# A two-layer mixer with a modulated block on one core: 256-byte tile lines, four-head latent queries, earlier output-gate panels, gating transposes in other banks

## The chip, the cores and the metric

The kernel runs on one core of one Trainium2 chip. The metric is the time of one execution on the device in microseconds (us). The kernel before was timed in 3 runs; their median is 2477.08 us, from 2476.04 to 2478.45.

## What is computed

512 tokens of width 1024 (fp32) go through two layers of one kind and one block of another. What matters here, cut from the reference:

```
def first_block(x, ...):                 # two layers
    for l in range(DEPTH):
        h = rmsnorm(x, g_pre_mix[l])
        (c_q, c_kv, k_r, p_in, s_u, s_v, cv_b, cv_c, cv_x, gate_logits) = split_cols(h @ w_in[l])
        y_a = mla_branch(c_q, c_kv, k_r, ...) @ w_br_a[l]      # q = rmsnorm(c_q) @ w_uq, 8 heads of 96
        y_b = pool_branch(p_in, ...) @ w_br_b[l]
        y_c = sgu_branch(s_u, s_v, ...) @ w_br_c[l]            # u * (masked 128 x 128 mix of rmsnorm(v))
        y_d = conv_branch(cv_b, cv_c, cv_x, ...) @ w_br_d[l]
        merged = sum of sigmoid(gate_logits) * (y_a, y_b, y_c, y_d)
        x = x + rmsnorm(merged @ w_out[l], g_post_mix[l])
        h = rmsnorm(x, g_pre_ffn[l])
        x = x + rmsnorm((silu(h @ w_ffn_gate[l]) * (h @ w_ffn_up[l])) @ w_ffn_down[l], g_post_ffn[l])

def second_block(x, c, ctx, c_ctx, w_mod, ...):
    sh1, sc1, g1, sh2, sc2, g2 = split(silu(c) @ w_mod + b_mod)     # and the same for c_ctx
    h = rmsnorm(x) * (1 + sc1) + sh1
    (q_na, k_na, v_na, q_g, k_g, v_g, og, z_lr, m_a, m_b) = split(h @ w_in)
    mix = merge(neighborhood attention(q_na, k_na, v_na), gated linear attention(q_g, k_g, v_g), silu(og), ...) @ w_out
    x = x + g1 * mix
    x = x + g2 * swiglu(modulated rmsnorm(x), w_ffn_gate, w_ffn_up, w_ffn_down)
```

## The kernel before, in words

The 512 tokens are 4 tiles of 128 rows, the width is 8 steps k of 128. Every large product is made of fp32r matmuls on operands split in a high and a low part (`split`): `mm3` issues three matmuls for each k, high x high, high x low, low x high. `fm` takes a weight panel as the stationary operand and the transposed activations as the moving one; `tm` the other way round. In the trace a matmul reads `out<-moving,stationary`: `pg<-wh,mTh` moves a weight panel over the stationary merged activations.

Weights come in panels of up to 128 x 1024 elements (`panel`, `wsplit`, L273 to L300): SP starts the load into one of 2 raw buffers `wr`, ACT casts it to `wh` (L261), DVE subtracts to get `wl` (L262); `wh` and `wl` have 4 buffers each. Work beside the main stream ("thread a") has raw buffers of its own, also 2, which it shares with the w_mod loads.

TensorE's order is written out: `inorder` (L247) chains every matmul and transpose to the one recorded before it. Side work is a list of items of several steps; `tick`, called every 4 k of a main product, lets the next steps in, 1.5 for a tick in the layers' mixing stage. The other engines' orders come from the scheduler, and each runs its own in order. PSUM has eight banks: `g` (3) for main products, `s` (2), `tp` (2) and `po` (1) for side work; `self.ps("t")` gives a main-stream caller a `g` bank, a side-work caller a `tp` bank.

A layer mixes in this order: latent projections; then the main stream computes conv, pool and SGU branches, each followed by its gate products and its branch product (`gates`; the branch output `brh`/`brl` is the moving operand), while MLA runs beside it: values, queries, keys, scores, softmax, probabilities times values, in four pairs of heads `hp` and four query tiles `j`. Queries (L755 to L784) load a 192-column panel of `w_uq` for each pair and make two calls, each for two token tiles: 2 x 2 x 3 matmuls of 192 columns. Scores (L802) read the pair's `qT`. Then `w_out` (`mTh`, `mTl` stationary) and the FFN; the last 8 of the 22 pairs of FFN activations lie in a pool `keep`, the others in `drop`. A generator with the modulation rows of the second block (L1066 on: load 128 x 512 of w_mod on SP, multiply-add on DVE, L1076 and L1078) fills in behind the MLA items and in the FFNs.

In the SGU branch `turned` transposes the gated halves, 8 transposes of 128 x 128, into two banks from `self.ps("t")` (L946), then splits them into `brh`/`brl`.

In the second block, keys and values of the neighborhood attention are projected in a loop over panels (L1168 to L1175); each value tile goes to DRAM (`vd`) in 8 writes of 32 rows on SP (L1540). Then four output-gate products follow, each with its panel requested right before it (L1182 to L1186).

Tiles come from pools through `Aligned.tile` (L94 to L111), which pads a tile's bytes in a partition to a multiple of 128. The pool of small constants adds up to 2688 bytes, ten and a half lines of 256, and pools stack on it.

Of the kernel before, what the change touches and what calls it, by code (L numbers as in the profile page):

```python
# [9 lines left out]
F32 = mybir.dt.float32  # L10
# [7 lines left out]
P = 128  # L18
# [21 lines left out]
CTX = 256  # L40
PHASE = 0
WARM = 12
HIGH = ((0, 0), (1, 0), (0, 1))
# [50 lines left out]
class Aligned:  # L94
# [5 lines left out]
    def tile(self, shape, dt, **kw):  # L100
        size = 2 if dt == BF16 else 4
        n = math.prod(shape[1:])
        if n * size % P == 0:
            return self.pool.tile(shape, dt, **kw)
        line = P // size
        t = self.pool.tile([shape[0], -(-n // line) * line], dt, **kw)[:, :n]
        if len(shape) == 2:
            return t
        names = "abc"[: len(shape) - 1]
        spaced = " ".join(names)  # L110
        return t.rearrange(f"p ({spaced}) -> p {spaced}", **dict(zip(names[1:], shape[2:])))  # L111


class Builder:
# [620 lines left out]
    def mla(self, l, o, q, kv):  # L735
# [18 lines left out]

        def queries(hp, t2):  # L755
            if t2 == 0:
                wqs[hp] = self.panel(a["w_uq"][l], 0, 2, hp * 192, 192)
                qTs[hp] = q.tile([QK, 2, SEQ], F32, name=self.nm("qT"), tag="qT", bufs=2)
            wq, qT = wqs[hp], qTs[hp]
            ps = self.ps()  # L760
            for i in range(2):
                ts = slice((2 * t2 + i) * P, (2 * t2 + i) * P + P)
                for k in range(2):
                    self.mm3(ps[:, i * 192 : i * 192 + 192], (cT[0][:, k, ts], cT[1][:, k, ts]), (wq[0][:, k], wq[1][:, k]), k == 0, k == 1)
            four = lambda x, d: x.rearrange("p (t h d) -> p t h d", t=2, h=2)
            v = four(ps[:, :384], QK)
            qn = self.f2()
            qv = four(qn[:, :384], QK)
            nc.scalar.activation(qv[:, :, :, :64], v[:, :, :, :64], AF.Copy, scale=QK ** -0.5)
            rt = self.f2()  # L770
            ra, rb = four(rt[:, :128], ROPE), four(rt[:, 128:256], ROPE)
            tab = lambda x, lo, hi: x[:, 2 * t2 : 2 * t2 + 2, None, lo:hi].to_broadcast([P, 2, 2, hi - lo])
            nc.vector.tensor_tensor(ra, v[:, :, :, 64:96], tab(Cq, 0, 32), op=ALU.mult)
            nc.vector.tensor_tensor(rb[:, :, :, :16], v[:, :, :, 80:96], tab(Sq, 0, 16), op=ALU.mult)
            nc.vector.tensor_tensor(rb[:, :, :, 16:], v[:, :, :, 64:80], tab(Sq, 16, 32), op=ALU.mult)
            nc.vector.tensor_tensor(qv[:, :, :, 64:96], ra, rb, op=ALU.add)

            def turn():
                pt = self.ps("t")
                for i in range(4):  # L780
                    self.transpose(pt[:QK, i * P : i * P + P], qv[:, i // 2, i % 2], ident)
                nc.scalar.copy(qT.rearrange("p h (t n) -> p t h n", t=NT)[:, 2 * t2 : 2 * t2 + 2], pt[:QK].rearrange("p (t h n) -> p t h n", t=2, h=2))

            pTs["q", hp, t2] = turn  # L784

# [11 lines left out]
        def scores(hp, j):  # L797
            n = (j + 1) * P
            ps = []
            for i in range(2):  # L800
                s = self.ps()
                self.matmul(s[:, :n], qTs[hp][:, i, j * P : j * P + P], kTs[hp][:, i, :n], start=True, stop=True)  # L802
                nc.vector.memset(s[:64, n - 64 : n], NEG)
                ps.append(self.softmax(q, s, n, 4))
            pTs[hp, j] = ps
# [21 lines left out]

        def project(hp):
            return [[do(queries, hp, t2), lambda: None, lambda t2=t2: pTs.pop(("q", hp, t2))()] for t2 in range(2)] + [[do(keys, hp)]]

        items = [[do(values, t)] for t in range(NT)] + project(0) + [[]]
        for hp in range(4):
            more = project(hp + 1) if hp < 3 else []
            for j in range(NT):
                items.append([do(scores, hp, j), lambda: None, do(probs, hp, j), do(values_of, hp, j)])
                if more:
                    items.append(more.pop(0))
        return items
# [66 lines left out]
    def sgu_branch(self, l, w_in, hT, brp, q):  # L905
# [38 lines left out]
        def turned():  # L944
            for m in range(2):
                pt = self.ps("t")  # L946
                for t in range(NT):
                    self.transpose(pt[:, t * P : (t + 1) * P], cs[:, t, m * P : (m + 1) * P], ident)
                self.split(cT[0][:, m], cT[1][:, m], pt)
# [164 lines left out]
    def block2(self, hT, before):  # L1114
# [53 lines left out]
        for name, c0 in (("k", 512), ("v", 1024)):  # L1168
            pans = self.pans(w_in, c0)
            for h, n, nt in ((hcT, name + "c", 2), (hT, name, NT)):  # L1170
                for t in range(nt):
                    ps = self.tm(h, pans, t, 512)
                    with self.thread("a"):
                        na[n](t, ps)
# [7 lines left out]
        for m in range(4):  # L1182
            ps = self.fm(hT, self.panel(w_in, 0, KD, 2560 + m * P, P), 0)
            nc.scalar.activation(og[m], ps, AF.Tanh, scale=0.5)
# [481 lines left out]
```

## Time and profile before

| what | before |
|---|---|
| median of 3 runs | 2477.08 us |
| profiled execution, its own time | 2477.62 us |
| its span | 2475.8 us |
| instructions in the span | 30539 |
| TensorE busy (matmul) | 2450.2 us, 99% |
| VectorE (DVE) busy | 1232.1 us, 50% |
| ScalarE (ACT) busy | 851.2 us, 34% |
| GpSimd (POOL) busy | 73.4 us, 3% |
| moved by DMA | 279.72 MB, mean 113 GB/s |

The profile times one execution. Its span is the time from the first to the last instruction recorded; the execution's own time is 1.8 us more. A busy share is an average over all stages. Matmuls overlap: the end of one is modelled and lies after the start of the next, so that the pace of a stream is read from start to start, not from the durations. "Idle before" in an instruction's row is the time its engine stood before it and what ended that.

### The profile page before, as it was taken

To read this page: it belongs to the slowest core of one execution; us is meant where nothing else is said; L and a number is where in the kernel's file an instruction comes from. 1 tells how busy PE (TensorE), PEld (TensorE's weight loads), DVE (VectorE), ACT (ScalarE), POOL (GpSimd) and SP (SyncE) were. 2 spreads that over 40 slices of the span, in tenths; PEclk is the share of its full clock that TensorE was granted. 3 is DMA by queue.
4 is the path that set the end of the run, shared out by engine and by line. 5 is a ranking of instruction groups with operands and counts; after the bars stand their busy time and mean duration, and the time that the engine had idled before them with its cause. 6 is when DMAs were issued, how large, how long until landed. Compare 5 with 4: busy or idle time off the path is not lost.

```text
span 2475.8 us, 30539 instructions
## 1 busy us (share of the span) xinstructions
PE 2450.2 (99%) x12155; PEld 2017.2 (81%) x12155; DVE 1232.1 (50%) x2018; ACT 851.2 (34%) x1414; POOL 73.4 (3%) x113
## 2 busy tenths in 40 slices
PE   9999999999999999999999999999999999999999
PEld 7877788988888887778898888877877778988887
DVE  6456544566522645554455443275535646543323
ACT  4343433322322434343332222244434533322211
POOL 1000000000000100000000000020100000000000
PEclk9999999999999999999999999999999999999999
DMA  5323334345424432443435333451133225333323
GB/s 160 92 75 110 105 94 153 119 136 174 134 94 141 128 96 79 123 124 94 153 111 154 101 96 104 141 179 48 55 94 120 69 69 170 111 94 97 99 94 128
DMA packets 339376, 279.72 MB, mean 113 GB/s; under 512 B 28262, under 2 KB 282430, under 8 KB 339233
## 3 DMA queue, kind: packets, MB, share of 16 engines
q1 hardware_dynamic: 339233, 277.76, 37.6%
q8 instruction: 96, 1.57, 0.3%
q14 instruction: 47, 0.39, 0.0%
HBM read 262.27 MB, written 15.45 MB: 112 GB/s over the span
## 4 chain that ended last, share of the span: by engine, by line
PE 61%; DVE 3%; ACT 1%; issue 1%; DMA 1%; POOL 0%; DVEq 0%; ACTq 0%; POOLq 0%; SPq 0%
PE pg L252 47%; PE ps L252 6%; PE ppo L252 3%; PE ptp L252 3%; PE ptp L255 2%; DVE wl L262 1%; DMA wr<-in_w_mod 1%; ACT wh L261 0%; POOL sm L337 0%; DVE hn L361 0%; ACT p L847 0%; DVE xt L412 0%; DVE hTl L262 0%; ACT jk L355 0%; DMA wr<-in_w_ffn_up 0%
## 5 line engine op out<-in xcount | busy, mean ns | idle before, releaser
L262 DVE TENSOR_TENSOR wl<-wr,wh 128x1024 fp32r<-128x1024 f32 (+1 forms) x392 | 463.6, 1184 | 739.2 <-ACT wh L261 719.1
L261 ACT CAST wh<-wr 128x1024 fp32r<-128x1024 f32 (+1 forms) x392 | 398.9, 1020 | 1063.3 <-issue 394.4
L252 PE MATMUL pg<-hTh,wh 128*128 128x512 f32 x1760 | 693.7, 394 | 3.2 <-ACT wh L261 2.1
L252 PE MATMUL pg<-hTh,wl 128*128 128x512 f32 x1760 | 682.3, 388 | 0.3 <-DVE wl L262 0.3
L252 PE MATMUL pg<-hTl,wh 128*128 128x512 f32 x1760 | 681.6, 387 | 0.0
L252 PEld LDWEIGHTS pg<-hTh,wh 128*128 128x128 f32 x1760 | 331.3, 188 | 75.5 <-issue 6.4
L252 PEld LDWEIGHTS pg<-hTh,wl 128*128 128x128 f32 x1760 | 331.1, 188 | 69.8 <-DVE wl L262 1.1
L252 PEld LDWEIGHTS pg<-hTl,wh 128*128 128x128 f32 x1760 | 331.5, 188 | 67.4 <-issue 2.4
L252 PE MATMUL pg<-wh,hTh 128*128 128x512 f32 (+2 forms) x288 | 113.6, 396 | 1.2 <-ACT wh L261 1.2
L252 PE MATMUL pg<-wl,hTh 128*128 128x512 f32 (+2 forms) x288 | 110.9, 387 | 3.3 <-DVE wl L262 3.3
L337 POOL TENSOR_TENSOR sm<-sm,misc 128x1 f32<-128x1 f32 (+3 forms) x72 | 58.8, 819 | 1745.2 <-DVE sm L336 1032.2
L252 PE MATMUL pg<-wh,hTl 128*128 128x512 f32 (+2 forms) x288 | 110.1, 384 | 0.0
L512 DVE TENSOR_TENSOR f<-f,pg 128x512 f32<-128x512 f32 x60 | 41.2, 686 | 122.0 <-PE pg L252 121.9
L1078 DVE SCALAR_TENSOR_TENSOR f<-wr,misc,f 128x512 f32<-128x512 f32 x112 | 81.3, 747 | 29.6 <-DMA wr<-in_w_mod 29.1
L847 ACT ACTIVATE p<-ps,sm 128x512 f32<-128x512 f32 (+3 forms) x96 | 55.7, 580 | 89.6 <-DVE sm L844 89.6
L252 PE MATMUL pg<-wh,al 128*128 128x512 f32 x198 | 77.3, 390 | 0.0
L252 PE MATMUL pg<-wl,ah 128*128 128x512 f32 x198 | 77.3, 390 | 0.0
L252 PE MATMUL pg<-wh,ah 128*128 128x512 f32 x198 | 77.3, 390 | 0.0
L252 PEld LDWEIGHTS pg<-wl,hTh 128*128 128x128 f32 x288 | 54.5, 189 | 16.2 <-DVE wl L262 6.0
L252 PEld LDWEIGHTS pg<-wh,hTh 128*128 128x128 f32 x288 | 54.5, 189 | 12.4 <-ACT wh L261 2.1
L252 PEld LDWEIGHTS pg<-wh,hTl 128*128 128x128 f32 x288 | 54.5, 189 | 10.2
L859 ACT COPY pT<-ptp 128x512 f32<-128x512 f32 (+3 forms) x96 | 41.5, 484 | 50.3 <-PE ptp L255 50.2
(361 smaller groups left out, 3605.7 us busy)
## 6 DMA issues: line engine op xcount, KB each, us to landing
wr<-in_w_in SPq DMA_DIRECT2D x128, 512.0 KB
wr<-in_w_ffn_gate SPq DMA_DIRECT2D x66, 512.0 KB
wr<-in_w_ffn_up SPq DMA_DIRECT2D x66, 512.0 KB
wr<-in_w_ffn_down SPq DMA_DIRECT2D x66, 512.0 KB
wr<-in_w_mod SPq DMA_DIRECT2D x96, 256.0 KB
wr<-in_w_out SPq DMA_DIRECT2D x24, 512.0 KB
xd<-xt SPq DMA_DIRECT2D x20, 512.0 KB
xt<-xd SPq DMA_DIRECT2D x20, 512.0 KB
```

The source lines that it names most:

```text
L252: self.inorder(self.nc.tensor.matmul(*args, **kw))
L255: self.inorder(self.nc.tensor.transpose(*args, **kw))
L261: h = (copy or nc.scalar.copy)(hi, src)
L262: l = nc.vector.tensor_tensor(lo, src, hi.bitcast(F32), op=ALU.subtract)
L337: nc.gpsimd.tensor_tensor(r, r, self.mhalf[:, :n], op=ALU.pow)
L512: nc.vector.tensor_tensor(t, t, ps, op=ALU.mult)
L847: nc.scalar.activation(p[:, :n], s[:, :n], AF.Exp, bias=nm, accum_out=sm)
L859: self.nc.scalar.copy(pT[:, :n], tp[:, :n])
L1078: nc.vector.scalar_tensor_tensor(acc, raw, sc, acc, op0=ALU.mult, op1=ALU.add)
```

## The change

Four edits, all in how work is laid out and ordered:

- Tiles are padded to multiples of 256 bytes instead of 128 (`LINE`), so that everything stacked on a padded tile stands at the same offset modulo 256.
- Queries are made for four heads and one token tile at a call: the panel of `w_uq` has 384 columns (loaded in two pieces, one for each k), a call has 2 x 3 matmuls of 384 columns, and `qT` holds four heads. The items of MLA are listed anew: the second four's queries and the keys of the pairs are interleaved with the scores by a table `more`.
- The four output-gate panels are requested in the loop of the value projection, ahead of the last value tile's writes.
- `turned` takes its two banks from `tp`.

```diff
--- before.py
+++ after.py
@@ -39,6 +39,7 @@
 WIN0 = (0, 8, 24, 32)
 CTX = 256
 PHASE = 0
+LINE = 256
 WARM = 12
 HIGH = ((0, 0), (1, 0), (0, 1))
 
@@ -100,9 +101,9 @@
     def tile(self, shape, dt, **kw):
         size = 2 if dt == BF16 else 4
         n = math.prod(shape[1:])
-        if n * size % P == 0:
+        if n * size % LINE == 0:
             return self.pool.tile(shape, dt, **kw)
-        line = P // size
+        line = LINE // size
         t = self.pool.tile([shape[0], -(-n // line) * line], dt, **kw)[:, :n]
         if len(shape) == 2:
             return t
@@ -752,36 +753,36 @@
                 self.mm3(ps[:, g * 256 : g * 256 + 256], (kvT[0][:, ts], kvT[1][:, ts]), wv[g], True, True)
             nc.scalar.copy(V[:, t], ps)
 
-        def queries(hp, t2):
-            if t2 == 0:
-                wqs[hp] = self.panel(a["w_uq"][l], 0, 2, hp * 192, 192)
-                qTs[hp] = q.tile([QK, 2, SEQ], F32, name=self.nm("qT"), tag="qT", bufs=2)
-            wq, qT = wqs[hp], qTs[hp]
+        def queries(f, t):
+
+            if t == 0:
+                wqs[f] = [self.panel(a["w_uq"][l], k, 1, f * 384, 384) for k in range(2)]
+                qTs[f] = q.tile([QK, 4, SEQ], F32, name=self.nm("qT"), tag="qT", bufs=2)
+            qT = qTs[f]
+            ts = slice(t * P, t * P + P)
             ps = self.ps()
-            for i in range(2):
-                ts = slice((2 * t2 + i) * P, (2 * t2 + i) * P + P)
-                for k in range(2):
-                    self.mm3(ps[:, i * 192 : i * 192 + 192], (cT[0][:, k, ts], cT[1][:, k, ts]), (wq[0][:, k], wq[1][:, k]), k == 0, k == 1)
-            four = lambda x, d: x.rearrange("p (t h d) -> p t h d", t=2, h=2)
+            for k, w in enumerate(wqs[f]):
+                self.mm3(ps[:, :384], (cT[0][:, k, ts], cT[1][:, k, ts]), (w[0][:, 0], w[1][:, 0]), k == 0, k == 1)
+            four = lambda x, d: x.rearrange("p (h d) -> p h d", h=4)
             v = four(ps[:, :384], QK)
             qn = self.f2()
             qv = four(qn[:, :384], QK)
-            nc.scalar.activation(qv[:, :, :, :64], v[:, :, :, :64], AF.Copy, scale=QK ** -0.5)
+            nc.scalar.activation(qv[:, :, :64], v[:, :, :64], AF.Copy, scale=QK ** -0.5)
             rt = self.f2()
             ra, rb = four(rt[:, :128], ROPE), four(rt[:, 128:256], ROPE)
-            tab = lambda x, lo, hi: x[:, 2 * t2 : 2 * t2 + 2, None, lo:hi].to_broadcast([P, 2, 2, hi - lo])
-            nc.vector.tensor_tensor(ra, v[:, :, :, 64:96], tab(Cq, 0, 32), op=ALU.mult)
-            nc.vector.tensor_tensor(rb[:, :, :, :16], v[:, :, :, 80:96], tab(Sq, 0, 16), op=ALU.mult)
-            nc.vector.tensor_tensor(rb[:, :, :, 16:], v[:, :, :, 64:80], tab(Sq, 16, 32), op=ALU.mult)
-            nc.vector.tensor_tensor(qv[:, :, :, 64:96], ra, rb, op=ALU.add)
+            tab = lambda x, lo, hi: x[:, t, None, lo:hi].to_broadcast([P, 4, hi - lo])
+            nc.vector.tensor_tensor(ra, v[:, :, 64:96], tab(Cq, 0, 32), op=ALU.mult)
+            nc.vector.tensor_tensor(rb[:, :, :16], v[:, :, 80:96], tab(Sq, 0, 16), op=ALU.mult)
+            nc.vector.tensor_tensor(rb[:, :, 16:], v[:, :, 64:80], tab(Sq, 16, 32), op=ALU.mult)
+            nc.vector.tensor_tensor(qv[:, :, 64:96], ra, rb, op=ALU.add)
 
             def turn():
                 pt = self.ps("t")
                 for i in range(4):
-                    self.transpose(pt[:QK, i * P : i * P + P], qv[:, i // 2, i % 2], ident)
-                nc.scalar.copy(qT.rearrange("p h (t n) -> p t h n", t=NT)[:, 2 * t2 : 2 * t2 + 2], pt[:QK].rearrange("p (t h n) -> p t h n", t=2, h=2))
-
-            pTs["q", hp, t2] = turn
+                    self.transpose(pt[:QK, i * P : i * P + P], qv[:, i], ident)
+                nc.scalar.copy(qT[:, :, ts], pt[:QK].rearrange("p (h n) -> p h n", h=4))
+
+            pTs["q", f, t] = turn
 
         def keys(hp):
             wk = self.panel(ukv, 0, 1, hp * 256, 256)
@@ -799,7 +800,7 @@
             ps = []
             for i in range(2):
                 s = self.ps()
-                self.matmul(s[:, :n], qTs[hp][:, i, j * P : j * P + P], kTs[hp][:, i, :n], start=True, stop=True)
+                self.matmul(s[:, :n], qTs[hp // 2][:, 2 * (hp % 2) + i, j * P : j * P + P], kTs[hp][:, i, :n], start=True, stop=True)
                 nc.vector.memset(s[:64, n - 64 : n], NEG)
                 ps.append(self.softmax(q, s, n, 4))
             pTs[hp, j] = ps
@@ -825,16 +826,17 @@
         def do(f, *args):
             return lambda: f(*args)
 
-        def project(hp):
-            return [[do(queries, hp, t2), lambda: None, lambda t2=t2: pTs.pop(("q", hp, t2))()] for t2 in range(2)] + [[do(keys, hp)]]
-
-        items = [[do(values, t)] for t in range(NT)] + project(0) + [[]]
+        def project(f):
+            return [[do(queries, f, t), lambda: None, lambda t=t: pTs.pop(("q", f, t))()] for t in range(NT)]
+
+        items = [[do(values, t)] for t in range(NT)] + project(0) + [[do(keys, 0)], []]
+        more = [[[do(keys, 1)]], project(1) + [[do(keys, 2)]], [[do(keys, 3)]], []]
         for hp in range(4):
-            more = project(hp + 1) if hp < 3 else []
             for j in range(NT):
                 items.append([do(scores, hp, j), lambda: None, do(probs, hp, j), do(values_of, hp, j)])
-                if more:
-                    items.append(more.pop(0))
+                if more[hp]:
+                    items.append(more[hp].pop(0))
+            items += more[hp]
         return items
 
     def softmax(self, q, s, n, bufs):
@@ -943,7 +945,7 @@
 
         def turned():
             for m in range(2):
-                pt = self.ps("t")
+                pt = self.bank("tp")
                 for t in range(NT):
                     self.transpose(pt[:, t * P : (t + 1) * P], cs[:, t, m * P : (m + 1) * P], ident)
                 self.split(cT[0][:, m], cT[1][:, m], pt)
@@ -1170,6 +1172,8 @@
             for h, n, nt in ((hcT, name + "c", 2), (hT, name, NT)):
                 for t in range(nt):
                     ps = self.tm(h, pans, t, 512)
+                    if n == "v" and t == NT - 1:
+                        pans = [self.panel(w_in, 0, KD, 2560 + m * P, P) for m in range(4)]
                     with self.thread("a"):
                         na[n](t, ps)
         self.drain()
@@ -1180,7 +1184,7 @@
         og = [q.tile([P, SEQ], F32, name=self.nm("og"), tag=f"og{m}") for m in range(4)]
         self.beside(self.gla_outputs(gla, og, zT, q), 1)
         for m in range(4):
-            ps = self.fm(hT, self.panel(w_in, 0, KD, 2560 + m * P, P), 0)
+            ps = self.fm(hT, pans[m], 0)
             nc.scalar.activation(og[m], ps, AF.Tanh, scale=0.5)
             nc.vector.scalar_tensor_tensor(og[m], og[m], 1.0, ps, op0=ALU.add, op1=ALU.mult)
             nc.vector.tensor_scalar(og[m], og[m], gla["gain"], 0.5, op0=ALU.mult, op1=ALU.mult)
```

The built program of the change puts the instructions as follows. Rows are in the order of their engine; the numbers in names are tile numbers.

On SP at the end of the value projection in the second block, before. `wr<-in_w_in 128x8x128` are the four output-gate panels and the panels after them; `vd` are the value writes, 8 for each token tile.

```order
L277 DMA wr_14633<-in_w_in 128x8x128
L277 DMA wr_14667<-in_w_in 128x8x128
L1540 DMA vd<-f_2752_14504 32x512 x8
L1540 DMA vd<-f_2754_14539 32x512 x8
L1540 DMA vd<-f_2756_14574 32x512 x8
L1540 DMA vd<-f_2758_14609 32x512 x8
L277 DMA wr_14712<-in_w_in 128x8x128
L277 DMA wr_14815<-in_w_in 128x8x128
```

And now:

```order
L278 DMA wr_14509<-in_w_in 128x8x128
L278 DMA wr_14515<-in_w_in 128x8x128
L1544 DMA vd<-f_2748_14404 32x512 x8
L1544 DMA vd<-f_2750_14439 32x512 x8
L1544 DMA vd<-f_2752_14474 32x512 x8
L278 DMA wr_14521<-in_w_in 128x8x128
L278 DMA wr_14527<-in_w_in 128x8x128
L1544 DMA vd<-f_2766_14533 32x512 x8
```

The third and fourth output-gate panel have moved ahead of the last 8 value writes.

On ACT at the same place, before. `wh<-wr` are the casts of the output-gate panels, `f<-pg` at L1536 the copy of a value tile, `og` the gates' activations, L1412 and L1413 work of the gated linear attention.

```order
L261 CAST wh_14634<-wr_14633 128x1024
L261 CAST wh_14668<-wr_14667 128x1024
L1536 COPY f_2758_14609<-pg_14584 128x512
L1184 ACTIVATE og_14629<-pg_14639 128x512
L1184 ACTIVATE og_14630<-pg_14673 128x512
L1412 ACTIVATE f_2776_14703<-ps_14698 128x512
L1413 ACTIVATE f_2777_14704<-ps_14698 128x512
L261 CAST wh_14713<-wr_14712 128x1024
L261 CAST wh_14816<-wr_14815 128x1024
```

And now:

```order
L262 CAST wh_14510<-wr_14509 128x1024
L262 CAST wh_14516<-wr_14515 128x1024
L1540 COPY f_2766_14533<-pg_14484 128x512
L1188 ACTIVATE og_14553<-pg_14557 128x512
L262 CAST wh_14522<-wr_14521 128x1024
L262 CAST wh_14528<-wr_14527 128x1024
L1188 ACTIVATE og_14554<-pg_14585 128x512
L1416 ACTIVATE f_2778_14615<-ps_14610 128x512
L1417 ACTIVATE f_2779_14616<-ps_14610 128x512
```

The casts of panels three and four now stand between the first and the second gate's activation; before they stood behind the second and the two copies after it.

The second place is SP in the MLA stage of layer 2, before. `wr<-in_w_in 128x2x512` are the four panels of the SGU projection, `wr<-in_w_mod` the modulation loads.

```order
L277 DMA wr_8592<-in_w_br_b 128x2x512
L1072 DMA wr_10713<-in_w_mod 128x512
L277 DMA wr_8607<-in_w_in 128x8x128
L277 DMA wr_8738<-in_w_in 128x2x512
L277 DMA wr_8744<-in_w_in 128x2x512
L277 DMA wr_8750<-in_w_in 128x2x512
L1072 DMA wr_10724<-in_w_mod 128x512
L1072 DMA wr_10727<-in_w_mod 128x512
L277 DMA wr_8756<-in_w_in 128x2x512
L1072 DMA wr_10738<-in_w_mod 128x512
```

And now, from the second load after the first SGU panel to the fourth panel:

```order
L1074 DMA wr_10624<-in_w_mod 128x512
L1074 DMA wr_10627<-in_w_mod 128x512
L1074 DMA wr_10638<-in_w_mod 128x512
L1074 DMA wr_10641<-in_w_mod 128x512
L278 DMA wr_8630<-in_w_in 128x2x512
L1074 DMA wr_10720<-in_w_mod 128x512
L278 DMA wr_8636<-in_w_in 128x2x512
L1074 DMA wr_10723<-in_w_mod 128x512
L1074 DMA wr_10797<-in_w_mod 128x512
L1074 DMA wr_10800<-in_w_mod 128x512
L1074 DMA wr_10803<-in_w_mod 128x512
L278 DMA wr_8642<-in_w_in 128x2x512
```

Before, 6 modulation loads of this stage stand ahead of the fourth SGU panel, and only 2 among the panels; now 13 stand ahead of it. In DVE's order 6 of a layer's 16 softmax pairs have modulation rows between or ahead of them before, 8 now.

## Rows read from the trace of the kernel before

**Rows 1.** The page: TensorE's busy time; the shares of the chain that ended last.

```profile
PE 2450.2 (99%) x12155; PEld 2017.2 (81%) x12155; DVE 1232.1 (50%) x2018; ACT 851.2 (34%) x1414; POOL 73.4 (3%) x113
...
PE 61%; DVE 3%; ACT 1%; issue 1%; DMA 1%; POOL 0%; DVEq 0%; ACTq 0%; POOLq 0%; SPq 0%
```

**Rows 2.** The chain's pieces in order of time: start us, us, what, matmuls.

```profile
824.30 6.82 PE pg L252 x36
...
1218.55 4.19 PE pg L252 x18
...
1512.35 4.08 PE pg L252 x18
...
1545.14 4.18 PE pg L252 x18
...
2108.02 5.75 PE pg L252 x48
2113.77 0.87 PE ptp L255 x8
...
2144.38 210.83 PE pg L252 x930
```

**Rows 3.** Timeline of TensorE, branch products: start us, us, line, operation, out<-in.

```profile
1139.13 0.40 PE L252 MATMUL pg<-brh,wh 128*128 128x512 f32 x1
...
1141.70 0.39 PE L252 MATMUL pg<-brh,wl 128*128 128x512 f32 x1
```

**Rows 4.** Timeline of TensorE, one call of the queries, its first matmul to the next.

```profile
220.34 0.34 PE L252 MATMUL ps<-wh,cTh 128*128 128x192 f32 x1
220.52 0.27 PE L252 MATMUL ps<-wl,cTh 128*128 128x192 f32 x1
...
221.75 0.42 PE L252 MATMUL pg<-hTh,wh 128*128 128x512 f32 x1
```

**Rows 5.** Timelines and windows (last column groups: PEclk, DMA share, GB/s), output-gate products.

```profile
1829.66 0.28 PE L252 MATMUL ps<-glal,glac 128*128 128x256 f32 x1
1832.06 0.79 PE L252 MATMUL pg<-hTh,wh 128*128 128x512 f32 x1 [2.12 <-ACT wh L261]
...
1833.61 0.80 PE L252 MATMUL pg<-hTh,wl 128*128 128x512 f32 x1 [0.34 <-DVE wl L262]
...
1839.71 0.39 PE L252 MATMUL pg<-hTh,wh 128*128 128x512 f32 x1
...
1832.00:1838.50 6.50, 6.11 (x15) 4.36 (x16) 2.69 (x4) 0.95 (x2) 0.00 (x0) 0.50 0.61 155
...
1830.95 2.00 ACT L261 CAST wh<-wr 128x1024 fp32r<-128x1024 f32 x2
...
1815.63 2.59 DVE L262 TENSOR_TENSOR wl<-wr,wh 128x1024 fp32r<-128x1024 f32 x2 [18.55 <-ACT wh L261]
...
1802.91 20.12 SPq L1540 DMA_DIRECT2D vd<-f  x32
```

**Rows 6.** Timeline of TensorE, the SGU transposes of layer 1 and the next matmul.

```profile
295.80 1.03 PE L255 MATMUL pg<-ident,su 128*128 128x128 f32 x8
297.36 0.50 PE L252 MATMUL pg<-hTh,wh 128*128 128x512 f32 x1 [0.53 <-ACT f L659]
```

**Rows 7.** MLA of layer 2: the costliest groups' row of w_mod's multiply-adds; timelines of DVE, PE, SP.

```profile
L1078 DVE SCALAR_TENSOR_TENSOR f<-wr,misc,f 128x512 f32<-128x512 f32 x112 | 81.3, 747 | 29.6 <-DMA wr<-in_w_mod 29.1
...
1053.46 0.75 DVE L1078 SCALAR_TENSOR_TENSOR f<-wr,misc,f 128x512 f32<-128x512 f32 x1 [1.91 <-DMA wr<-in_w_mod]
...
1054.85 0.88 PE L252 MATMUL ppo<-pT,V 128*64 128x128 f32 x12
...
1058.37 0.48 PE L252 MATMUL pg<-wh,hTh 128*128 128x512 f32 x1
...
1030.65 0.38 SPq L277 DMA_DIRECT2D wr<-in_w_in  x1
...
1047.81 0.39 PE L252 MATMUL pg<-wh,hTh 128*128 128x512 f32 x1
```

## The prediction

> **What bounds the kernel now.** I read the page first: TensorE is busy 99% of the span and 61% of the chain that ended last is its work [rows 1]. So a change counts only where it shortens TensorE's own stream or takes away a place where TensorE waits. Next I read the pace of that stream from the chain, dividing a piece's time by its matmuls (pieces by their start). Block 2's FFN (2144.38) goes through 930 matmuls of 512 columns at 210.83 / 930 = 226.7 ns each. FFN-down of layer 2 runs at 4.08 / 18 = 226.7 ns (1512.35) and then, 33 us later in the same loop, at 4.18 / 18 = 232.2; w_out of layer 2 (1218.55) at 4.19 / 18 = 232.8 [rows 2]. In the program as built, the slow ones have one operand at a byte offset of 0 modulo 256 (`mT` of the two layers, and the last 8 of their 22 FFN activations, those in the pool `keep`), the fast ones both at 128. The gating products of the branches (`brh`, `brl` at offset 0) go from 1139.13 to 1141.70 in 11 steps, 233.6 ns each [rows 3]. I found nothing else that parts the two kinds: same lines, same shapes, same engines around them. Last I read the timeline at the other three edits: the query matmuls [rows 4], the output-gate stall [rows 5], the SGU transposes [rows 6], and the MLA stage, whose order of work moves [rows 7].
>
> **1. Whole 256-byte lines.** No instruction is added or removed by this edit; operands move. Of 8,958 matmuls with 512 fp32r columns, 7,812 have both operands at offset 128 before. In the change 8,922 have, 1110 more: 384 of w_out, 384 of FFN-down, 288 of `br` and 50 small ones. 768 x 5.5 ns [rows 2] = 4.2 us; 288 x 5 ns = 1.4 (less than the difference of 233.6 to 226.7, since other matmuls of that busy stage stand a little above 226.7 too); the 50 others 0.2. All of it is on TensorE's path: **5.8 us**. Bounds: nothing, if the address is not the cause, and 1110 x 6.9 ns = 7.7. A loss I exclude: the 930 matmuls of block 2 already run in the arrangement that all get. Padding costs space, no instruction.
>
> **2. Queries of four heads.** In both layers 16 calls of 12 matmuls with 192 columns become 16 calls of 6 with 384; rotations, copies, transposes and panel bytes stay the same in number and size. One call takes 221.75 - 220.34 = 1.41 us, and its steps are 1.23 / 11 = 112 ns [rows 4]. That is well above what 192 columns would take in proportion to 512 (85 ns), so something other than columns sets it. Before: 16 x 1.41 = 22.6 us. For 384 columns no row exists; between 256 columns at 5.75 / 48 = 119.8 and 512 at 226.7 [rows 2] a straight line gives 173.3 ns. After: 96 x 173.3 = 16.6, and 16 x 0.07 for the longer first step of a call = 1.1, so 17.7. **4.9 us** gained. Bounds: at the 416-column pace of the latent projection, 6.82 / 36 = 189.4 (824.30, [rows 2]), 3.3 us; in proportion to 512 columns (170 ns), 5.2. The straight line is taken because 256 and 512 enclose 384 at two known paces. The Trainium skill (TensorE: Matmul & The Clock Gate, Back-to-back issue gap) gives for a lone matmul N / 2.4 + 2.5 ns, so an estimate of 82.5 ns for 192 columns and 162.5 for 384, by which this edit would be worth 192 x 82.5 - 96 x 162.5 = 0.2 us. The rows disagree at 192 (112 measured).
>
> **3. Output-gate panels.** Before, og panel 2 stands on SP behind 32 value writes that go out from 1802.91 to 1823.03, its cast on ACT starts at 1830.95, behind what ACT does for og panel 1, and TensorE idles 2.12 us for it and 0.34 for its low part [rows 5]. Then the granted clock is 0.50 (1.2 GHz of 2.4) to 1838.5 although TensorE works. From 1829.78, when the matmul before could be followed, to 1839.71, 9.93 us go by for 12 matmuls of 512 columns (2.72 us), 8 transposes (0.87, [rows 2]) and 4 matmuls of 256 (0.48): 4.07 at the fast level. 5.86 are lost, 2.5 as waits and the rest to the clock. After, panels 2 and 3 are requested ahead of the last 8 value writes, and the casts on ACT ahead of the second og panel's activation. The buffer of panel 2 comes free when DVE has made the low part of og panel 0, by 1818.2 [rows 5], while 24 writes at 20.12 / 32 = 0.63 us end at 1818.0; so SP waits for nothing new. The load takes no longer than from its request after 1823.03 to its cast at 1830.95, 7.9 us; so by 1826.1 it is there, by then ACT is done with og panel 0 (its 24 matmuls end one panel, 5.4 us, before 1829.78), and cast and low part (1.0 and 1.3 us) are through at 1828.4, over 1 us ahead of need. Behind the two panels on SP wait only 8 value writes, which are read again some 50 us later. Late next would be panel 3, whose cast comes 1.1 us after that of panel 2 and is needed 2.7 us after it. I take off 0.15 for a remaining bubble: **5.7 us**. Bounds: 0 (panel as late as now) and 5.9. That the clock stays at 2.4 GHz without the idle stretch is the part not shown; without it 2.5 remain.
>
> **4. SGU transposes in other banks.** Eight transposes take 0.87 us where nothing is in the way [rows 2] and 297.36 - 295.80 = 1.56 here, since the matmuls behind them want the bank that ACT still reads [rows 6]; layer 2 repeats it. With the transposes in a bank of their own the next main product has a bank that was freed earlier. 2 x 0.69 = **1.4 us**, bounds 0 and 1.6 (the first matmul after is slow too).
>
> **5. MLA in another order.** All queries now end one head pair earlier, and so the modulation rows (w_mod loads, DVE multiply-adds) begin earlier: 8 of 16 softmax pairs of a layer have them ahead on DVE, before 6. DVE runs in order, and a multiply-add that waits for its load holds the softmax behind it. This has happened once in 12 such pairs: DVE waits 1.91 us at 1053.46, and 12 small matmuls and 4 score matmuls take from 1054.85 to 1058.37, some 2.4 us too long (1.7 to 2.8, by what one counts as their own) [rows 7]. Per pair that is 0.2 us, for 16 pairs 0.8 more than now, within what I leave out: 0, bounds a gain of 2.4 (this stall goes) and a loss of 4.8 (two more). On SP, the last of the four SGU panels now stands behind 13 w_mod loads of this stage, each of which waits for DVE, where 6 stood ahead of it. It goes out at 1030.65 now and is used at 1047.81 [rows 7]. By the new order of DVE some four multiply-adds stand between each two gating products, which come 9 to 11 us apart, and the load that frees SP for this panel is worked off beside the same gating product as now. So I cost it at nothing behind a cover of 17 us less a load and its cast (7.9 + 2.3); if that cover fails it is some 2 us a load (DVE's wait of 1.91).
>
> **Sum.** 5.8 + 4.9 + 5.7 + 1.4 = 17.8 us off the profiled 2477.62, 2459.8; the median of the runs is 0.5 lower. Forecast **2459.5 us**.
>
> **The rivals.**
> *A: the address is not the cause.* Then the 768 matmuls stay at 232 ns for another reason, perhaps what DVE and ACT do just then. For: in the mixing stage matmuls with both operands at 128 are also a little slow, while DVE and ACT are busy. Against: block 2 runs the same loops at 226.7. Time 2459.5 + 5.8 = 2465.3. The Trainium skill (SBUF — State Buffer, Specifications) speaks of 16-byte cachelines; by that rule offsets of 0 and 128 are alike and this rival holds. [Rows 2] speak against it.
> *B: wide query matmuls cost in proportion to narrow ones*, twice 112 ns. Then 96 x 224 + 1.1 = 22.6 us, nothing gained: 2459.5 + 4.9 = 2464.4. Against: 256 columns cost 119.8, hardly more than 192. By the page's formula for the gap (above) it would come to 2464.2.
> *C: the gate stall only moves*, as SP holds the two panels until a buffer is free and ACT casts them no earlier, or the clock falls anyhow: between 2459.5 + 3.2 and + 5.7, 2465.2.
> *D, slower: w_mod loads hold the softmaxes in both layers.* Place: head pairs 2 and 3 of MLA, DVE. A load comes about 2 us after DVE is ready for it, as at 1053.46, ahead of most of the 16 pairs. Price 2.4 us for each pair. It decides from the tenth pair on: (17.6 + 5) / 2.4 = 9.4. With 12 of 16, 11 more than now, 2459.5 + 26.4 = 2486. Against: 11 of 12 pairs get through now, and all waits of DVE for these loads come to 29.1 us over 112 instructions [rows 7], mostly outside MLA.
> *E: the change does not do what it says*, in that A, B and C hold together: 2459.5 + 5.8 + 4.9 + 5.7 = 2475.9, no change.
>
> **How the numbers follow.** Forecast 0.54; A 0.15; B 0.07; C 0.10; two of these at once (2470 to 2471) 0.05; E 0.04; D 0.05. The forecast's own ends are 7.7 + 5.2 + 5.9 + 1.6 + 2.4 = 22.8 off, 2454.5, and, with 3.3 for the queries and a loss of 4.8 in MLA, 2466. Runs of this kernel lie 1.2 us around their median, so the low end is 2453. The high end takes in A, B and C and ends at 2470, where two of them together begin; these, E and D, 0.14, lie outside. 0.2%, 5 us, is about what a measurement of this kernel can tell from no change: faster means under 2472. Faster 0.90, same 0.05, slower 0.05.
>
> **What would show it.** In the profile after: pieces of 18 matmuls in the chain at 4.08 throughout w_out and FFN-down of both layers (A wrong), `br` products under 230 ns; 384-column steps of 170 to 176 ns (B wrong); no wait for ACT at the third og panel and a granted clock of 1.00 there (C wrong); 0.9 us for eight `su` transposes. The prediction is wrong if DVE rows waiting for w_mod stand right ahead of softmax rows with score matmuls idle behind them more than twice, or if the SGU stage opens with a wait for a panel.

## The result and the profile after

The changed kernel takes 2461.64 us (median of 4 runs, 2461.35 to 2461.97), the kernel before 2477.46 in the same comparison (4 runs). The ratio is 0.9937 with a 95% interval of 0.9919 to 0.9954: 15.8 us faster, between 11.4 and 20.1. The forecast was 2459.5, in a range of 2453 to 2470. In a second comparison on another chip (e5 below) the gain was 14.1 us. The profiled execution took 2461.91 us with a span of 2460.1.

The page of the changed kernel, its busy times and the shares of the chain that ended last (before: [rows 1]; line numbers are one to two higher):

```profile
PE 2437.1 (99%) x12059; PEld 2011.1 (82%) x12059; DVE 1232.7 (50%) x2018; ACT 849.5 (35%) x1414; POOL 73.0 (3%) x113
...
PE 46%; DVE 2%; ACT 1%; DMA 1%; issue 1%; POOL 0%; SPq 0%; ACTq 0%; DVEq 0%; POOLq 0%
```

TensorE has 96 matmuls less and is as busy as before. Its share of the last chain fell from 61% to 46%, but the other shares did not grow: all listed add up to 67% before and 51% now. The pieces of the chain go back to 802 us in the kernel before and only to 1232 us here, so the fall says how far back the chain could be followed, not what limits the kernel.

The start of the same matmul in both traces tells where the time went. On the left stands the stretch by its times in the kernel before, on the right by how much it became shorter (-) or longer (+):

| stretch before, us | what runs there | change, us |
|---|---|---|
| 0 to 401 | layer 1: latents, MLA, conv, pool, SGU, gates | -3.92 |
| 401 to 460 | w_out of layer 1 | -1.05 |
| 460 to 495 | its end: norms and transposes for the FFN | +0.53 |
| 495 to 866 | FFN of layer 1 with its end | -0.23 |
| 866 to 1207 | layer 2: the same as in layer 1 | -5.42 |
| 1207 to 1255 | w_out of layer 2 | -0.92 |
| 1255 to 1303 | its end | +0.60 |
| 1303 to 1622 | FFN of layer 2 | -0.93 |
| 1622 to 1660 | its end, start of the second block | +1.18 |
| 1660 to 1821 | projections of the second block | +0.24 |
| 1821 to 1851 | output gates | -5.83 |
| 1851 to the end | rest of the second block | +0.02 |

They add up to -15.73, the difference of the spans. Each part of the change is in it, and in four places behind w_out and FFN-down time comes back. The seven rows of w_out, FFN and their ends add up to -0.82 only. Rows of some tenths are to be read with care: in e3 below, which changes nothing before the second block, the first 30 us came out 0.59 us longer and the stretch from 1255 to 1303 0.38 shorter than in the profile of the kernel before.

**The pace.** The chain's pieces of layer 2's FFN-down and the second block's FFN (before: [rows 2]):

```profile
1501.88 4.08 PE pg L253 x18
...
1534.52 4.08 PE pg L253 x18
...
2128.63 210.83 PE pg L253 x930
```

The piece that took 4.18 takes 4.08, the block that was in the good arrangement before is the same to the hundredth. The branch products (before: [rows 3]) go from 1128.67 to 1131.61 in 13 steps, 226 ns each instead of the 233.6 before:

```profile
1128.67 0.39 PE L253 MATMUL pg<-brl,wh 128*128 128x512 f32 x1
...
1131.61 0.39 PE L253 MATMUL pg<-brh,wl 128*128 128x512 f32 x1
```

**One call of the queries** (before: [rows 4]), three of its six matmuls on TensorE's timeline; the first step is 0.26 us, the others 0.17 to 0.18:

```profile
156.50 0.42 PE L253 MATMUL ps<-wh,cTh 128*128 128x384 f32 x1
156.76 0.34 PE L253 MATMUL ps<-wl,cTh 128*128 128x384 f32 x1
...
157.46 0.35 PE L253 MATMUL ps<-wh,cTl 128*128 128x384 f32 x1
```

**The output gates** (before: [rows 5]) on TensorE's timeline: the matmul ahead of the third panel, its first one, the first one after it. Then the window around them, with PEclk, DMA share and GB/s at its end:

```profile
1819.72 0.28 PE L253 MATMUL ps<-glal,glac 128*128 128x256 f32 x1
1819.85 0.40 PE L253 MATMUL pg<-hTh,wh 128*128 128x512 f32 x1
...
1823.94 0.39 PE L253 MATMUL pg<-hTh,wh 128*128 128x512 f32 x1
```

```profile
1815.00:1825.00 10.00, 10.00 (x54) 8.51 (x53) 5.66 (x9) 4.97 (x9) 0.00 (x0) 1.00 0.40 105
```

From 1819.85 to 1823.94, 4.09 us for what took 9.93, without a wait and at a granted clock of 1.00.

**The SGU transposes** (before: [rows 6]): 0.79 us to the next matmul instead of 1.56.

```profile
293.01 1.03 PE L256 MATMUL ptp<-ident,su 128*128 128x128 f32 x8
293.80 0.48 PE L253 MATMUL pg<-hTh,wh 128*128 128x512 f32 x1
```

**MLA** (before: [rows 7]). The group of the score matmuls, before and then after (last the idle time ahead of them), and the row of the timeline where TensorE waits instead:

```profile
L252 PE MATMUL ps<-kT,qT 96*128 96x128 f32 (+3 forms) x128 | 40.9, 439 | 2.0 <-ACT p L847 2.0
```

```profile
L253 PE MATMUL ps<-kT,qT 96*128 96x128 f32 (+3 forms) x128 | 40.5, 437 | 0.1
```

```profile
1040.02 0.50 PE L253 MATMUL pg<-wl,hTh 128*128 128x512 f32 x1 [0.73 <-DVE wl L263]
```

In this execution the softmax no longer keeps the scores waiting; in the second profile of the same kernel (e5) the scores still wait 0.9 us in all. TensorE waits 0.73 us for the low part of the fourth SGU panel instead. ACT had finished that panel's cast at 1036.56; DVE came to the low part only behind softmax and gate products:

```profile
1036.41 0.42 DVE L852 TENSOR_SCALAR p<-p,sm 128x384 f32<-128x384 f32 x1
...
1038.22 0.62 DVE L675 TENSOR_TENSOR merged<-merged,f 128x512 f32<-128x512 f32 x1
1038.76 1.21 DVE L263 TENSOR_TENSOR wl<-wr,wh 128x1024 fp32r<-128x1024 f32 x1
```

Two multiply-adds of w_mod run on DVE from 1030.06 on, the first behind a wait of 0.48 us for its load. That they are what makes DVE late here fits the order of work, but no run takes them away, so it is not shown.

### The profile page after: what moved, and what is told of

It reads as the page before. It is cut to its first block, busy times and chain, and to the rows that moved or that the text cites. A ratio compares the mean times of both kernels' runs of the same rounds, so it can differ in the third digit from the quotient of the medians.

```text
span 2460.1 us, 30349 instructions
## 1 busy us (share of the span) xinstructions
PE 2437.1 (99%) x12059; PEld 2011.1 (82%) x12059; DVE 1232.7 (50%) x2018; ACT 849.5 (35%) x1414; POOL 73.0 (3%) x113
## 3 DMA queue, kind: packets, MB, share of 16 engines
q8 instruction: 95, 1.56, 0.3%
## 4 chain that ended last, share of the span: by engine, by line
PE 46%; DVE 2%; ACT 1%; DMA 1%; issue 1%; POOL 0%; SPq 0%; ACTq 0%; DVEq 0%; POOLq 0%
PE pg L253 35%; PE ps L253 4%; PE ptp L253 3%; PE ppo L253 3%; PE ptp L256 1%; DVE wl L263 1%; ACT wh L262 0%; DMA xt<-xd 0%; ACT p L849 0%; DMA wr<-in_w_in 0%; DMA wr<-in_w_ffn_gate 0%; DVE hn L362 0%; DVE hTl L263 0%; DVE xt L413 0%; POOL sm L338 0%
```

## The experiments

The first four put each edit alone into the kernel before, on one chip (before there: 2476.20 us, 33 runs from 2473.16 to 2479.08).

**e1, lines of 256 bytes alone.**

```diff
-        if n * size % P == 0:
+        if n * size % LINE == 0:
...
-        line = P // size
+        line = LINE // size
```

> The kernel before with the line of 256 bytes alone. Theory (the pace follows the operands' offsets, but the ends of w_out and FFN-down are held by DVE and ACT, so that part of the gain is given back there): all 512-column matmuls of w_out, FFN-down and the branch products at 227 ns instead of 232, worth 5.9 us of TensorE's own work, of which some 3 us come back as waits at the four ends of w_out and FFN-down: 2.5 to 3.5 us faster. Rival (nothing is given back): 5.5 to 6 us faster. Rival (the offset is not the cause, the gain came with the new order of work): no difference, paces of 232 stay.

Measured: 2472.40 us, ratio 0.9984 (0.9975 to 0.9992), 3.8 us faster. In the trace w_out of layer 1 is 1.06 us shorter and its end 1.25 longer; all of FFN-down's pieces in the chain (layer 2) run at 4.08. So the offset is the cause of the pace, and part of what it gives is lost at the ends. The gain is a little above what was expected, and its interval, 2.0 to 6.2 us, also holds the rival by which nothing is given back; against that rival speak the traces. This row of TensorE's timeline is the end of w_out in layer 1, a wait of 1.59 us for DVE, below it the same place in the kernel before:

```profile
460.52 0.66 PE L256 MATMUL ptp<-ident,hn 128*128 128x128 f32 x4 [1.59 <-DVE hTl L263]
```

```profile
460.90 0.66 PE L255 MATMUL ptp<-ident,hn 128*128 128x128 f32 x4 [0.34 <-DVE hTl L262]
```

**e2, queries of four heads alone.** From its edit, which is the queries' part of the diff above:

```diff
-                wqs[hp] = self.panel(a["w_uq"][l], 0, 2, hp * 192, 192)
+                wqs[f] = [self.panel(a["w_uq"][l], k, 1, f * 384, 384) for k in range(2)]
```

> The kernel before with the four-head queries and the new list of MLA items alone. Theory: the query matmuls themselves 4.0 us shorter (21.9 to 17.9 us), and the stall of 2.4 us at the softmax of layer 2 gone since the modulation rows fall otherwise: 6 to 6.5 us faster, score matmuls wait for nothing. Rival (the stall went for another reason): 4 us faster and the stall still there. Rival (MLA's new order costs elsewhere): under 3 us.

Measured: 2472.35 us, ratio 0.9983 (0.9974 to 0.9992), 3.9 us faster; the profiled span 5.1 shorter, 2.7 in each layer's mixing. The wait of the scores is 0.4 us instead of 2.0, so most of it does go with the new order; but TensorE waits 1.12 us for the SGU panel in its place. The 6 to 6.5 us expected did not come, and the net is near what the query matmuls give alone:

```profile
1044.57 0.50 PE L252 MATMUL pg<-wl,hTh 128*128 128x512 f32 x1 [1.12 <-DVE wl L262]
```

**e3, the output-gate panels alone.**

```diff
+                    if n == "v" and t == NT - 1:
+                        pans = [self.panel(w_in, 0, KD, 2560 + m * P, P) for m in range(4)]
...
-            ps = self.fm(hT, self.panel(w_in, 0, KD, 2560 + m * P, P), 0)
+            ps = self.fm(hT, pans[m], 0)
```

> The kernel before with the output-gate panels requested ahead of the last value writes alone. Theory: 5.8 us faster, no idle time ahead of the third output-gate panel, the granted clock 1.00 through it. Rival (the clock falls there whatever happens, and after's clock stayed up for another of the edits): 2.5 us faster, granted clock 0.5 for some 6 us.

Measured: 2471.19 us, ratio 0.9980 (0.9971 to 0.9989), 5.0 us faster; the stretch of the gates itself is 5.84 shorter, as in the changed kernel. The group of TensorE's main matmuls has lost its 2.1 us of waiting for ACT's casts, and keeps the 1.1 of the SGU (before, then here):

```profile
L252 PE MATMUL pg<-hTh,wh 128*128 128x512 f32 x1760 | 693.7, 394 | 3.2 <-ACT wh L261 2.1 <-ACT f L659 1.1
```

```profile
L252 PE MATMUL pg<-hTh,wh 128*128 128x512 f32 x1760 | 692.5, 393 | 1.1 <-ACT f L659 1.1
```

**e4, the SGU transposes alone.**

```diff
-                pt = self.ps("t")
+                pt = self.bank("tp")
```

> The kernel before with the SGU transposes in the other banks alone. Theory: 0.7 us in each layer, 1.4 us faster; eight transposes to the next matmul 0.9 us instead of 1.56. Rival (the wait moves to the bank's next user): under 0.5 us.

Measured: 2475.02 us, ratio 0.9994 (0.9985 to 1.0003), 1.2 us faster, not clear of zero by itself. In the trace each layer's place is 0.76 and 0.79 us shorter. The profiled execution lost 1.6 us elsewhere, in MLA of layer 2: the windows of that stage (PEclk third from the end), before and then here, show the granted clock below 1 behind the same wait of the scores.

```profile
1030.00:1075.00 45.00, 43.03 (x222) 33.65 (x221) 34.18 (x78) 18.15 (x47) 1.66 (x3) 1.00 0.52 160
```

```profile
1030.00:1075.00 45.00, 43.17 (x215) 33.38 (x214) 32.92 (x77) 16.68 (x45) 1.66 (x3) 0.96 0.51 155
```

A mean of 0.96 over 45 us means 3.6 us at half speed, so 1.8 lost. The profiles of e1 and e9, which have the same wait, show 0.96 too; those of the kernel before and e3, which also have it, show 1.00. So behind the stall that the prediction priced at 2.4 us some executions lose another 1.8 to the clock and others do not; why is not shown.

The next four ran together on another chip (before there: 2475.40 us, 9 runs).

**e5, the changed kernel again.**

> The changed kernel again, to stand beside the three others on the same chip: 14 to 16.5 us faster than the kernel before.

Measured: 2461.28 us (2460.52 to 2463.80), ratio 0.9942 (0.9929 to 0.9956), 14.1 us faster. The four edits alone give 3.8 + 3.9 + 5.0 + 1.2 = 13.9, which agrees with 14.1 as far as these runs can tell (each of the four has an interval of some 2 us to either side).

**e6, everything at offset 0.** All pools are pushed by 128 bytes:

```diff
-        for side, n in ((None, PHASE), ("right", 96 - PHASE)):
+        for side, n in ((None, 128), ("right", 224)):
```

> The changed kernel with everything pushed by 128 bytes, so that both operands of 8,922 matmuls of 512 columns stand at offset 0 modulo 256 instead of 128. Theory (what costs is that the two operands differ modulo 256): paces of 227 ns as in the changed kernel, the same time within 1 us. Rival (offset 0 itself is slow): 8,922 x 5.5 ns = 49 us slower than the changed kernel. Rival (only a stationary operand at 0, or only a moving one, is slow): the same 49 us, since both are at 0.

Measured: 2460.89 us (2460.41 to 2462.53), the same as e5. The chain's piece at the place that was slow before:

```profile
1534.63 4.08 PE pg L253 x18
```

Offset 0 is not slow. What costs is that one operand stands at 0 and the other at 128, and either way round: in the slow matmuls of the kernel before the stationary operand is at 0 in w_out [rows 2] and the moving one in the branch products [rows 3].

**e7, 768 matmuls with unlike offsets.** In the changed kernel two pools, those of the layers' merged activations and of their last FFN activations, get a pad of 128 bytes (cut: `keep` is shown, the pool of `mT` gets it in the same way, and a switch turns it on in the layers alone):

```diff
+    def shifted(self, pool):
+        if self.shift:
+            pad = pool.pool.tile([P, 32], F32, name=self.nm("sh"), tag="sh")
+            self.nc.gpsimd.memset(pad, 0.0)
+        return pool
...
-        keep = self.pool("actk", 1, stack=ks)
+        keep = self.shifted(self.pool("actk", 1, stack=ks))
```

> The changed kernel with the two layers' merged activations and the last 8 pairs of their FFN activations pushed by 128 bytes: 768 matmuls of w_out and FFN-down get unlike offsets again, nothing else moves. Theory (the ends of w_out and FFN-down wait for DVE and ACT, which took back part of the gain): TensorE's stream is 768 x 5.6 ns = 4.3 us longer, the kernel only 1 to 2.5 us slower than the changed one, with less waiting of TensorE at the ends. Rival (what came back had another cause): 4.3 us slower.

Measured: 2464.14 us (2462.56 to 2464.38), 2.9 us slower than e5, a little more than expected and less than 4.3. The ranges of the two, five runs each, overlap, so the times alone do not part 2.9 from 4.3. The traces do: w_out and FFN with their ends are together 1.1 and 1.3 us longer than in the two traces of the changed kernel, where the matmuls became 4.3 us slower. The slow pieces are back where the padded activations are used:

```profile
1525.15 4.08 PE pg L254 x18
...
1530.60 4.19 PE pg L254 x18
```

And the wait at the end of FFN-down of layer 2 is short again: the transposes of a normalised tile, here, then in the changed kernel, with the window around the latter:

```profile
1613.15 1.32 PE L257 MATMUL pg<-ident,hn 128*128 128x128 f32 x8 [0.32 <-DVE hn L365]
```

```profile
1611.89 1.32 PE L256 MATMUL pg<-ident,hn 128*128 128x128 f32 x8 [1.67 <-DVE hn L364]
```

```profile
1611.00:1619.00 8.00, 7.07 (x28) 5.64 (x29) 7.22 (x13) 3.74 (x7) 2.91 (x2) 0.79 0.28 87
```

DVE is busy 7.22 of these 8 us, and was nearly as busy there in the kernel before:

```profile
1622.00:1630.00 8.00, 7.86 (x38) 6.28 (x38) 7.12 (x14) 3.86 (x7) 3.49 (x3) 1.00 0.28 84
```

It sets the pace of the end (e10 below takes work from it); the faster TensorE waits 1.35 us longer for it. The granted clock then averages 0.79, where e7 and the kernel before stay at 1.00.

**e8, one step more.** The context's low-rank projection goes behind its key products, where TensorE waits for late value panels:

```diff
-        gla["lrc"](self.lows(hcT, lpan))
-        ds = ExitStack()
-        self.beside(gla["decays"](self.pool("decay", 1, stack=ds, side="right")), 1)
         for t in range(2):
             gla["kc"](t, self.tm(hcT, pans, t, 256, 256))
         pans = self.pans(w_in, 2048)
+        gla["lrc"](self.lows(hcT, lpan))
+        ds = ExitStack()
+        self.beside(gla["decays"](self.pool("decay", 1, stack=ds, side="right")), 1)
```

> The changed kernel with one more step moved: in the second block the context's low-rank projection (24 matmuls of 256 columns, 2.9 us) runs after the context's key products instead of ahead of them, so that it stands where TensorE now idles 0.7 and 3.1 us for the context value panels, after which the granted clock is 0.62 for 4.5 us. Theory (a panel that comes late costs its wait and then the clock, as at the output gates): 4 to 5 us faster than the changed kernel. Rival (the load is late by as much again, since its buffers come free no earlier): 0 to 1 us.

Measured: 2460.14 us (2459.52 to 2463.07), 1.1 us faster than e5, with ranges that overlap. It is the lowest median of all kernels here, but no more than that. Against the two traces of the changed kernel its own shows 4.0 to 5.1 us gained at the place itself and 3.0 to 3.3 lost at the next panels, 36 us later: TensorE waits for the key panels of the neighborhood attention, 1.40 and 0.77 us, and the granted clock falls there now.

```profile
1720.60 0.49 PE L253 MATMUL pg<-wh,hTh 128*128 128x512 f32 x1 [1.40 <-ACT wh L262]
1721.86 0.50 PE L253 MATMUL pg<-wl,hTh 128*128 128x512 f32 x1 [0.77 <-DVE wl L263]
```

```profile
1720.00:1735.00 15.00, 13.51 (x60) 10.72 (x61) 5.31 (x8) 5.16 (x7) 1.65 (x1) 0.89 0.32 95
```

In the changed kernel the same place has waits of 0.58, 0.76 and 0.43 us and a clock of 1.00. Most of the stall was only moved.

**e9 and e10, lighter ends.** In the kernel before and in the changed one the tails leave out the addition of the shift row:

```diff
-                hns[t] = self.norm(q, xs[t], g, b, self.turned_at[0] if t == 2 else None)
+                hns[t] = self.norm(q, xs[t], g, None, self.turned_at[0] if t == 2 else None)
```

> The kernel before without the addition of the shift row to the normalised tile in the tails that feed the second block (end of layer 2, middle of the block): DVE has 1.29 us less for each of the four tiles there. Theory (DVE holds these ends): 1 to 3 us faster than the kernel before, TensorE waits less for the normalised tiles. Rival (TensorE's stream holds them): the same time as before within 0.5 us.

> The changed kernel with the same addition left out. Theory (at the end of layer 2 the gain of the offsets was given back to DVE): TensorE's 1.67 us of waiting there shrink below 0.7, the granted clock stays 1.00, and from the last FFN-down of layer 2 to the second block's first products the gain over the kernel without the addition is kept to 0.5 us, where the changed kernel lost 1.3 us of it. Rival (the loss there had another cause, such as the loads of xt): the same 1.3 us are lost.

Measured, on a third chip (before there: 2476.03 us, 15 runs): e9 2477.34 us, ratio 1.0004 (0.9994 to 1.0013), not faster; e10 2460.87 us, ratio 0.9942 (0.9929 to 0.9954). In neither does TensorE wait for a normalised tile at the end of layer 2 any more. In e10 the clock stays at 1.00, and the stretch from 1622 to 1660 is 0.71 us shorter than before instead of 1.18 longer. That part went as expected. In e9 the stretch is 0.68 longer, against what was expected: a wait comes up behind the one removed, for DVE's work on the second block's queries, and the clock falls (0.83 over 10 us):

```profile
1640.53 0.63 PE L255 MATMUL ptp<-ident,f 128*128 128x128 f32 x4 [1.21 <-DVE f L1504]
```

```profile
1640.00:1650.00 10.00, 8.68 (x37) 7.08 (x38) 5.03 (x9) 3.64 (x8) 2.60 (x2) 0.83 0.47 159
```

The same wait comes up in e10, and there it is even longer, but the clock stays at 1.00:

```profile
1629.25 0.63 PE L256 MATMUL ptp<-ident,f 128*128 128x128 f32 x4 [1.38 <-DVE f L1508]
```

```profile
1629.00:1639.00 10.00, 8.96 (x47) 7.47 (x48) 5.90 (x11) 4.92 (x13) 3.28 (x2) 1.00 0.51 157
```

So what parts the two is not this wait but the clock behind it. e9's profiled execution was also the slowest of its 11 runs (2479.63 us) and has the clock of 0.96 in MLA; why the clock fell in one and not in the other is not shown.

## Why the prediction was right, and where it was off

The sign and the mechanisms of the four edits were right: 15.8 us measured, 17.6 forecast against the median. Rivals A, B and C fell (paces, 175 ns, clock of 1.00), D and E with them. By its steps:

1. *Lines of 256 bytes, forecast 5.8 us.* The pace came as said. The count holds but for the small ones: 48 of the 50 have both operands at offset 0 in the kernel before as built, so that by e6 they had nothing to gain (0.2 us of the term), and 48 of those counted as at 128 start at 160 or 224, in both kernels alike; e6 shows that likeness and not the offset itself decides. The step that failed is "All of it is on TensorE's path". Alone the edit gave 3.8 us. In the changed kernel's trace w_out and FFN with their ends gave 0.82 us, where the term has 4.2 for their 768 matmuls. The ends of w_out and FFN-down wait for DVE, which the page's 50% for DVE does not tell and the window does (7.22 of 8 us). Four ends gave back 0.5, 0.6, 0.6 and 1.2 us in the profiled execution; e7 shows the other side of the same, 768 slower matmuls cost 2.9 of 4.3 us. That DVE is what gives it back is shown by experiment at the end of layer 2 (e10); at the other three it is read from the waits. The prediction went by TensorE's idle time, in all small, and not by how near to late each end stood. The Trainium skill (SBUF — State Buffer, Specifications) names cachelines of 16 bytes, by which offsets of 0 and 128 would be alike. e6 agrees where both operands share the offset; where they do not, [rows 2] and e7 show 5.5 ns of 227.

2. *Queries, forecast 4.9.* They gave 4.0: all query matmuls together took 21.96 us from start to start before and 17.93 after. The forecast for after, 17.7, held; 384 columns step at 175 ns within a call, 173.3 were taken from the straight line. The term for before, 16 x 1.41 = 22.6, was too large, since the one call shown was slower than the mean of 1.37. The Trainium skill's formula for a lone matmul (TensorE: Matmul & The Clock Gate, Back-to-back issue gap) would have made the edit worth 0.2 us; neither of the steps estimated from it, 82.5 and 162.5 ns, is what these rows show (112 and 175).

3. *Output-gate panels, forecast 5.7.* 5.83, with the part that was "not shown", the clock, as forecast. This was the best known term: everything in it stood in the trace.

4. *SGU transposes, forecast 1.4.* 0.76 and 0.79 in e4's trace, 1.55. TensorE's row of the main product behind them has no wait any more.

5. *MLA, forecast 0 between a gain of 2.4 and a loss of 4.8.* The scores wait 0.1 us in one trace of the changed kernel and 0.9 in the other (e5) instead of 2.0; a wait of 0.7 to 1.1 for the low part of the last SGU panel came. Without what queries, branch products and SGU transposes gave, the mixing of layer 2 is about 1 to 2 us shorter in these two traces. The prediction named a wait for a panel at the opening of the SGU stage as a sign of being wrong; a wait did come, at the stage's fourth panel, and it was smaller than what the other waits lost. The prediction costs that panel by its load on SP; it was late on DVE.

So the sum was 1.8 us too good, and that it came so near is in part luck. In the changed kernel's trace w_out and FFN gave 3.4 us less than their share of the first term, while the two mixing stages gave 9.3 where queries, SGU transposes and branch products together have 7.7: two misses of opposite sign.

What stays open: why the three runs shown of before lay within 2.4 us and 33 later ones spread over 5.9. The clock in MLA of layer 2 (0.96 in three profiled executions with the old order of MLA, e1, e4 and e9; 1.00 in two, the kernel before and e3) accounts for 1.8 of it and was not followed further.

## What to carry to other kernels

Before you count a faster stream as time, look at each place where the stream ends, and read there in a window of a few us how busy the engine is that takes over: an average of 50% can hide 90%. A wait that you remove frees time only down to the next wait behind it, and a wait of 1 to 2 us may cost as much again in granted clock (2.5 us of waits and 3.4 of clock at the output gates, nothing behind 1.38 us in e10), so both belong in the price. And look at where operands stand: 128 bytes of padding decided on 2% of a matmul's pace.

## What was not expected of the hardware

- A 512-column fp32r matmul with one operand at byte offset 0 and the other at 128 modulo 256 takes 5.5 ns more than with like offsets (4.18 against 4.08 us for 18). Both at 128 and both at 0 run alike (2461.28 and 2460.89 us).
- The granted clock fell to its lower level behind waits of quite different length: after 2.12 us at the output gates (0.50 for 6.5 us), 1.67 at the end of layer 2 (0.79 over 8 us), 1.21 and 0.80 in e9 (0.83 over 10 us), but not after 1.38 and 0.80 at the same place in e10 (1.00); and behind the wait of the scores in MLA, 0.7 and 1.1 us, in some executions (0.96 over 45 us in e4) and not in others (1.00 in the kernel before).
- A query matmul of 192 columns steps at 112 ns, one of 384 at 175; other fp32r matmuls step at 119.8 with 256: from 256 columns to 192 the step shrinks by 8 ns only.
